# A hybrid decoder layer: fewer expert tiles ahead, and the router's queries in two passes

## The chip, the cores and the metric

The kernel runs on one core of a Trainium2 chip. It holds one layer of a decoder trunk for 512 tokens of width 2048 in float32. The metric is the device time of one execution in microseconds. The kernel before takes 3278.4 us (median of three runs, 3274.56 to 3291.7).

## What is computed

The layer adds two things to its input `h`: attention, and a layer of very small experts (PEER). A final norm follows. The change touches the second part alone. Per token it is:

```python
q = (xt @ w_query).reshape(T, 8, 2, 128)               # 8 heads, two halves
scores = jnp.einsum('thpc,hpnc->thpn', q, sub_keys)    # 128 keys for each half
vals, idx = lax.top_k(scores, 16)                      # of each half
cand = (vals[..., 0, :, None] + vals[..., 1, None, :]).reshape(T, 8, 256)
top_vals, top_c = lax.top_k(cand, 16)                  # 16 experts a head, 128 a token
experts = i1 * 128 + i2                                # of 16384
gates = softmax(top_vals)
hdn = gelu(einsum('ted,td->te', expert_down[experts], x))
y = einsum('ted,te->td', expert_up[experts], gates * hdn)
```

## The kernel before, in words

**Two ways to the experts.** Tokens come in four blocks of 128. The first 320 tokens go through *all* 16384 experts on TensorE, and a table `g_d` of gates, zero nearly everywhere, picks what counts. The last 192 tokens (64 of block 2, part "e", and all of block 3, part "g") are *gathered*: an indirect DMA on Pool (L511) brings one expert row for each of 128 partitions, 1 MB, and DVE multiplies and sums it (L517 for the down table, L525 for the up table). There are 384 such steps (`steps`, 64 down and 64 up for "e", 128 and 128 for "g"); four row buffers (`NROW`) hold what is under way.

**Weights in two halves.** Each float32 weight tile (128x1024, 512 KB) is rounded on ACT to a high part (L93) and the rest is a low part (L94, by DVE or Pool as `lo_on` says); `mm3` makes three matmuls of it (L99 to L101). A *down tile* is 128 experts: two pieces, 48 matmuls of 320 columns (`dn`), then Gelu into `hold`. An *up* step is 24 matmuls (`up`), 16 steps for a group of eight experts' tiles.

**Stages.** Behind attention, h is normed and transposed (`ht`). *Routing*: `queries(hp)` makes one half of one head's queries for all 512 tokens (48 matmuls of 512 columns, `pq`), the part for blocks 0 and 1 is set aside in `kept`; `choose(hh, b0, ...)` then searches two blocks on DVE (L541 to L545 top 16, L578 to L580 the one-hot lookup of the index). Calls for blocks 2 and 3 alternate with calls for blocks 0 and 1 one head behind. *One-hot stage*: for 40 groups of eight tokens, DVE makes two one-hot tiles (L673, L674), ACT scales one, PE multiplies them (`gm`, L680), ACT copies to `stg`, and SP writes `g_d`; one gather step goes with each group. Since PE has room there, `SPILL` = 28 down tiles (experts 100 to 127) are computed ahead and parked in DRAM (`hid_d`), and then ten more into the ten `hold` buffers. *Loop*: up steps for group g, one down tile every two steps, and gather steps by a rate (`due`, 1.6 a step while there are down tiles and 0.8 later, when `hold` is reloaded from `hid_d`). The last group of eight brings in the final norm.

**What sets the order.** The code is written in program order, and a scheduler places instructions on each engine by its own estimate, within what buffers and dependences allow. Every engine then works strictly in that order, and so does the queue of SP, which issues the loads: an instruction that waits holds all behind it.

Of the kernel before, what the change touches and what calls it, by code (L numbers as in the profile page):

```python
# [18 lines left out]
P = 128  # L19
# [10 lines left out]
PH = 8  # L30
# [14 lines left out]
ER = P // NE  # L45
EH = 128 // ER
HOLD = 10
SPILL = 28
NG = 8

PACE = mybir.DependencyInfo(mybir.DependencyClass.NoSync, mybir.DependencyReason.SCHED_ONLY)
# [8 lines left out]
def peer_block(ctx, tc, x, x_t, w_qk, w_v, w_fg, w_o, w_pq, sub_keys, down_t, down, up_t, up,  # L60
# [17 lines left out]
    ahead = []  # L78

    def fetch(src, pool):  # L80
        raw = pool.tile([P, 1024], F32, tag="raw", name="raw", bufs=3)
        DMA.dma_start(raw, src)
        return raw

    def load_split(src, lo_on=None, pool=None, bufs=2):

        pool = pool or wts
        raw = ahead.pop(0) if ahead else fetch(src, pool)
        if isinstance(raw, tuple):
            return raw  # L90
        hi = pool.tile([P, 1024], F32R, tag="hi", name="hi", bufs=bufs)
        lo = pool.tile([P, 1024], F32R, tag="lo", name="lo", bufs=bufs)
        A.activation(hi, raw, AF.Copy)  # L93
        (lo_on or V).tensor_tensor(lo, raw, hi.bitcast(F32), ALU.subtract)  # L94
        return hi, lo
# [343 lines left out]
    def aux(name):  # L439
        return psum.tile([P, S], F32, tag="aux", name=name, bufs=4)  # L440
# [91 lines left out]
    with tc.tile_pool(name="route", bufs=1, side="right") as rp:  # L532
# [57 lines left out]
                V.reciprocal(den, den)  # L590
                V.tensor_tensor(t, t, den.unsqueeze(2).broadcast_to([P, RB * PH, TK]), ALU.mult)

        kept = rp.tile([P, 2 * PH, RB * P], F32, name="kept")

        def queries(hp):
            ps = aux(f"pq{hp}")
            for piece in range(2):
                hi, lo = load_split(w_pq[hp, :, piece * 1024:(piece + 1) * 1024], G if hp else V)
                for kk in range(8):
                    k = piece * 8 + kk  # L600
                    sl = slice(kk * P, (kk + 1) * P)
                    mm3(ps, (hi[:, sl], lo[:, sl]), (hn[0][:, :, k], hn[1][:, :, k]), k == 0, k == NK - 1)
            qt = rp.tile([P, RB * P], F32, name="qt", bufs=2)
            A.copy(qt, ps[:, RB * P:])
            A.copy(kept[:, hp], ps[:, :RB * P])
            return qt


        for hh in range(PH):
            choose(hh, NB - RB, queries)  # L610
            if hh == PH - 1:
                for dst, src in ((gidx_e, ex), (gate_e, top)):
                    for r in range(ER):
                        V.tensor_copy(dst[r * NE:(r + 1) * NE], src[E0:, EB].rearrange("p h k -> p (h k)")[:, r * EH:(r + 1) * EH])
                V.tensor_copy(gidx, ex[:, GB])
                V.tensor_copy(gate_g, top[:, GB].rearrange("p h k -> p (h k)"))
            if hh:
                choose(hh - 1, 0, lambda hp: kept[:, hp])
        choose(PH - 1, 0, lambda hp: kept[:, hp])
    if "ex" in dbg:  # L620
        DMA.dma_start(dbg["ex"], ex)
        DMA.dma_start(dbg["gate"], top)
# [69 lines left out]
    with tc.tile_pool(name="exp", bufs=1, side="right") as xp:  # L692
# [110 lines left out]
        for g in range(NE1 // NG):  # L803
            pp = []
            for j in range(NG):
                e = g * NG + j
                ph, pl = (z[:, NGC:].rearrange("p c k t -> p (c k t)")[:, pslot * ND:(pslot + 1) * ND] for z in hn)
                pslot = (pslot + 1) % npslot
                A.activation(ph, hold[e], AF.Copy)
                V.tensor_tensor(pl, hold[e], ph.bitcast(F32), ALU.subtract)  # L810
                pp.append((ph, pl))
            for c in range(NK):
                uh, ul, _ = ups.pop(0)
                ps = aux("up")
                for j in range(NG):
                    mm = mm3(ps[:, :ND], (uh[:, j], ul[:, j]), pp[j], j == 0, j == NG - 1)
                up_split(g * NK + c + 1)
                if g == 0:
                    add = V.tensor_copy(yacc[:, c], ps[:, :ND])
                else:  # L820
                    add = V.tensor_tensor(yacc[:, c], yacc[:, c], ps[:, :ND], ALU.add)
                behind = ups[0][2] if ups else None
                if ups:
                    tc.add_manual_dep(add.ins, behind, PACE, reason="pace")
                e = HOLD + g * NG + c // 2
                if c % 2 and e < NE1:
                    if e < NE1 - SPILL:
                        down_tile(e, (V, V))
                    else:
                        hold[e] = hold_p.tile([P, ND], F32, tag="hold", name=f"hold{e}")  # L830
                        DMA.dma_start(hold[e], hid_d[e - (NE1 - SPILL)])
                if c % 2 and (g + 1) * NG + c // 2 < NE1:
                    gate_tile((g + 1) * NG + c // 2)
                due += 1.6 if e < NE1 - SPILL else 0.8
                while due >= 1:
                    gather_step(mm, behind)
                    due -= 1
                if g == NE1 // NG - 1 and c == NK - 1:
                    assert gstep[0] >= len(steps)
                if g == NE1 // NG - 2 and c == 4:  # L840
                    fin_load()
                if g == NE1 // NG - 1 and c % 4 == 3:
                    fin_quarter(c // 4)
# [74 lines left out]
```

## Time and profile before

| | |
|---|---|
| median of three runs | 3278.4 us |
| the profiled execution | 3290.1 us, its span 3288.3 us |
| mean granted TensorE clock | 0.976 |
| PE, DVE, ACT, POOL busy | 94%, 75%, 37%, 30% of the span |
| moved by DMA | 846 MB, 402.7 MB of it by the gathers |
| routing, one-hot stage | 966 to 1232 us, 1242 to 1478 us |
| loop from the first up step to the last down tile | 1642 to 2936 us |
| up steps alone, last group and norm | 2936 to 3288 us |

The table gives the stages by the times at which their first and last instructions stand. A busy share over the whole span hides that the bound changes from stage to stage; it is read stage by stage.

### The profile page before, as it was taken

What the parts mean: (1) busy time and instruction counts of PE and PEld (TensorE: products, weight loads), DVE (VectorE), ACT (ScalarE), POOL (GpSimd) and SP (SyncE); (2) the same over time, 40 slices, a digit from 0 to 9 for tenths busy, and PEclk for the clock granted to TensorE, in tenths of its full rate; (3) what the DMA queues carried; (4) which work ended last, traced back from release to release, by engine and by line L of the source; (5) the groups of instructions that cost most, each with busy time, mean ns of one, the idle gap of its engine ahead of it and who ended that gap; (6) DMA issues with size and microseconds to landing.
All of it is one profiled execution on the core that took longest, in us unless ns stands there. A gap on an engine that the chain in (4) does not pass through costs nothing.

```text
span 3288.3 us, 46948 instructions
## 1 busy us (share of the span) xinstructions
PE 3099.4 (94%) x18265; PEld 2830.5 (86%) x18265; DVE 2472.8 (75%) x3518; ACT 1211.2 (37%) x1849; POOL 971.8 (30%) x515
## 2 busy tenths in 40 slices
PE   6999999999999968889999998999999999998897
PEld 4887778878877767789999998999999999988887
DVE  5226665444348999980799998999999999988895
ACT  4224444343231127883333333333333333322233
POOL 2000000000013346775434433334434333432210
PEclk9999999999999998989999999999999999999998
DMA  4322222224442237986799999999999999999883
GB/s 179 101 93 75 69 69 73 66 66 129 134 135 71 77 122 256 339 325 235 279 387 392 395 404 333 405 406 379 386 402 404 404 395 406 383 380 361 326 328 123
DMA packets 215791, 846.49 MB, mean 257 GB/s; under 512 B 20944, under 2 KB 69456, under 8 KB 163216
## 3 DMA queue, kind: packets, MB, share of 16 engines
q1 hardware_dynamic: 159424, 439.37, 37.2%
q0 software_dynamic: 55296, 402.68, 30.8%
q8 instruction: 143, 2.34, 0.3%
q10 hardware_dynamic: 848, 1.44, 0.2%
q14 instruction: 80, 0.66, 0.1%
HBM read 806.31 MB, written 35.91 MB: 256 GB/s over the span
## 4 chain that ended last, share of the span: by engine, by line
PE 75%; DVE 12%; DMA 4%; POOL 4%; issue 4%; ACT 1%; ACTq 0%; SPq 0%; POOLq 0%; DVEq 0%
PE dn L99 8%; PE up L99 8%; PE dn L100 8%; PE up L100 7%; PE up L101 7%; PE dn L101 7%; PE mm L101 4%; PE mm L100 4%; PE mm L99 4%; POOL lo L94 2%; PE po L100 2%; PE po L99 2%; PE po L101 2%; PE gm L680 2%; PE pv L101 2%
## 5 line engine op out<-in xcount | busy, mean ns | idle before, releaser
L93 ACT ACTIVATE hi<-raw 128x1024 fp32r<-128x1024 f32 x416 | 440.4, 1059 | 750.7 <-PE dn L101 206.0
L99 PE MATMUL dn<-hn,lo 128*128 128x320 f32 x2048 | 653.6, 319 | 62.5 <-POOL lo L94 62.0
L99 PE MATMUL up<-hn,ulo 128*128 128x320 f32 x2048 | 645.6, 315 | 43.6 <-DVE ulo L797 43.4
L94 DVE TENSOR_TENSOR lo<-raw,hi 128x1024 fp32r<-128x1024 f32 x320 | 389.6, 1224 | 375.6 <-ACT hi L93 375.0
L100 PE MATMUL dn<-hn,hi 128*128 128x320 f32 x2048 | 647.7, 316 | 0.0
L100 PE MATMUL up<-hn,uhi 128*128 128x320 f32 x2048 | 640.3, 313 | 6.3 <-DVE hn L810 6.3
L101 PE MATMUL dn<-hn,hi 128*128 128x320 f32 x2048 | 645.6, 315 | 0.0
L101 PE MATMUL up<-hn,uhi 128*128 128x320 f32 x2048 | 639.1, 312 | 0.0
L796 ACT ACTIVATE uhi<-uraw 128x1024 fp32r<-128x1024 f32 x256 | 271.5, 1061 | 638.2 <-PE up L101 482.8
L99 PEld LDWEIGHTS dn<-hn,lo 128*128 128x128 f32 x2048 | 389.7, 190 | 74.0 <-POOL lo L94 72.4
L99 PEld LDWEIGHTS up<-hn,ulo 128*128 128x128 f32 x2048 | 390.4, 191 | 57.4 <-DVE ulo L797 52.9
L100 PEld LDWEIGHTS up<-hn,uhi 128*128 128x128 f32 x2048 | 390.8, 191 | 7.9 <-DVE hn L810 7.9
L101 PEld LDWEIGHTS up<-hn,uhi 128*128 128x128 f32 x2048 | 390.4, 191 | 0.0
L100 PEld LDWEIGHTS dn<-hn,hi 128*128 128x128 f32 x2048 | 390.1, 190 | 0.0
L101 PEld LDWEIGHTS dn<-hn,hi 128*128 128x128 f32 x2048 | 389.1, 190 | 0.0
L94 POOL TENSOR_TENSOR lo<-raw,hi 128x1024 fp32r<-128x1024 f32 x96 | 274.4, 2865 | 293.5 <-ACT hi L93 293.5
L797 DVE TENSOR_TENSOR ulo<-uraw,uhi 128x1024 fp32r<-128x1024 f32 x256 | 313.5, 1225 | 57.7 <-ACT uhi L796 57.5
L511 POOL DMA_INDIRECT rows<-in_up,gidx x128 | 214.5, 1676 | 408.4 <-DVE yg_g L525 392.4
L511 POOL DMA_INDIRECT rows<-in_down,gidx x128 | 227.2, 1775 | 357.7 <-DVE rows L517 324.7
L517 DVE SCALAR_TENSOR_TENSOR rows<-rows,hng_g 128x2048 f32<-128x2048 f32 x128 | 290.4, 2283 | 9.9 <-DMA rows<-in_down,gidx 5.9
L525 DVE SCALAR_TENSOR_TENSOR yg_g<-rows,coef_g,yg_g 128x2048 f32<-128x2048 f32 x127 | 297.7, 2344 | 0.0
L108 POOL TENSOR_TENSOR rstd_g<-ms_g,mhalf 128x4 f32<-128x4 f32 x2 | 2.0, 1016 | 685.5 <-DVE ms_g L106 685.5
(257 smaller groups left out, 5132.3 us busy)
## 6 DMA issues: line engine op xcount, KB each, us to landing
raw<-in_down_t SPq DMA_DIRECT2D x256, 512.0 KB
uraw<-in_up_t SPq DMA_DIRECT2D x256, 512.0 KB
raw<-in_w_qk SPq DMA_DIRECT2D x64, 512.0 KB
g_d<-stg SPq DMA_DIRECT2D x10, 2048.0 KB
gt<-g_d SPq DMA_DIRECT2D x32, 640.0 KB
raw<-in_w_v SPq DMA_DIRECT2D x32, 512.0 KB
raw<-in_w_o SPq DMA_DIRECT2D x32, 512.0 KB
raw<-in_w_pq SPq DMA_DIRECT2D x32, 512.0 KB
```

The source lines that it names most:

```text
L93: A.activation(hi, raw, AF.Copy)
L94: (lo_on or V).tensor_tensor(lo, raw, hi.bitcast(F32), ALU.subtract)
L99: PE.matmul(ps, a[1], b[0], start=first, stop=False)
L100: PE.matmul(ps, a[0], b[1], start=False, stop=False)
L101: return PE.matmul(ps, a[0], b[0], start=False, stop=last)
L108: G.tensor_tensor(r[:, :width], m[:, :width], mhalf[:, :width], ALU.pow)
L511: ld = G.indirect_dma_start(out=rows, out_offset=None, in_=table, in_offset=bass.IndirectOffsetOnAxis(ap=ix[:, j:j + 1], axis=0))
L517: use = V.scalar_tensor_tensor(rows, rows, 1.0, hng[part], ALU.mult, ALU.mult, accum_out=dots[part][:, j:j + 1])
L525: use = V.scalar_tensor_tensor(yg[part], rows, coef[part][:, j:j + 1], yg[part], ALU.mult, ALU.add)
L680: gm = PE.matmul(ps[:, t * P:(t + 1) * P], o2[:, qq * 4 + t], o1[:, qq * 4 + t], start=True, stop=True)
L796: A.activation(uh, raw, AF.Copy)
L797: sub = V.tensor_tensor(ul, raw, uh.bitcast(F32), ALU.subtract)
```

## The change

`SPILL` goes from 28 to 8: experts 120 to 127 are computed ahead, and the loop has down tiles up to 119. Queries are made twice: once for blocks 2 and 3, all heads, and then for blocks 0 and 1, so that `kept` is not needed, each matmul has 256 columns, and the query weights are loaded, rounded and subtracted in both passes. They have buffers of their own in the pool of routing (`rp`), two raw ones. In the first pass DVE makes the low part of each first piece and Pool of each second (both on DVE for the very first half); in the second Pool makes all but the first half's. The index lists of the gathered tokens are complete behind the first pass, and two gather steps follow each call of the second. The rate in the loop goes to 1.38 and 0.65 a step.

```diff
-SPILL = 28
+SPILL = 8
...
-        raw = pool.tile([P, 1024], F32, tag="raw", name="raw", bufs=3)
+        raw = pool.tile([P, 1024], F32, tag="raw", name="raw", bufs=3 if pool is wts else 2)
...
-        kept = rp.tile([P, 2 * PH, RB * P], F32, name="kept")
-
-        def queries(hp):
-            ps = aux(f"pq{hp}")
...
+        def queries(b0):
+
+            def of(hp):
+                ps = aux(f"pq{hp}{b0}")[:, :RB * P]
+                cg = slice(b0 * P // GC, (b0 + RB) * P // GC)
+                for piece in range(2):
+                    hi, lo = load_split(w_pq[hp, :, piece * 1024:(piece + 1) * 1024], G if hp and (piece or b0 == 0) else V, rp)
+                    for kk in range(8):
+                        k = piece * 8 + kk
+                        sl = slice(kk * P, (kk + 1) * P)
+                        mm = mm3(ps, (hi[:, sl], lo[:, sl]), (hn[0][:, cg, k], hn[1][:, cg, k]), k == 0, k == NK - 1)
+                qt = rp.tile([P, RB * P], F32, name="qt", bufs=2)
+                A.copy(qt, ps)
+                last[0] = mm
+                return qt
+            return of
...
         for hh in range(PH):
-            choose(hh, NB - RB, queries)
...
-            if hh:
-                choose(hh - 1, 0, lambda hp: kept[:, hp])
-        choose(PH - 1, 0, lambda hp: kept[:, hp])
+            choose(hh, NB - RB, queries(NB - RB))
...
+        for hh in range(PH):
+            choose(hh, 0, queries(0))
+            for _ in range(2):
+                gather_step(last[0])
...
-                due += 1.6 if e < NE1 - SPILL else 0.8
+                due += 1.38 if e < NE1 - SPILL else 0.65
```

What the scheduler makes of it, at three places. On PE, at the end of the one-hot stage, before (`gm` are the one-hot products, `dn` down tiles):

```order
L680 MATMUL gm<-o_10120,o_10119 128x128
L101 MATMUL dn_11185<-hn_6788,hi 128x320
L99 MATMUL dn_11185<-hn_6788,lo 128x320
L100 MATMUL dn_11185<-hn_6789,hi 128x320
L101 MATMUL dn_11185<-hn_6788,hi 128x320
```

And at the same place now:

```order
L683 MATMUL gm<-o_11105,o_11104 128x128 x8
L683 MATMUL gm<-o_11132,o_11131 128x128 x8
L683 MATMUL gm<-o_11159,o_11158 128x128 x8
L99 MATMUL up<-hn_6788,ulo 128x320
L100 MATMUL up<-hn_6789,uhi 128x320
```

Counted in that order, 809 matmuls of down tiles stood ahead of the last one-hot product, and 1015 more between it and the first up step. Now 138 stand ahead of the first query, 289 among the queries, 629 from there to the last one-hot product, and none between it and the first up step.

On DVE, just ahead of the low part of the first up weights, now (`rows` gather products, `hold` gate products, `ulo` the low part); before, the low part stood there without any gate product ahead of it:

```order
L517 SCALAR_TENSOR_TENSOR rows_12039,dots_e<-rows_12039,hng_e 128x2048
L785 TENSOR_TENSOR hold_11773<-hold_11773,gt_12375 128x320
L785 TENSOR_TENSOR hold_11839<-hold_11839,gt_12375 128x320
L785 TENSOR_TENSOR hold_11905<-hold_11905,gt_12375 128x320
L517 SCALAR_TENSOR_TENSOR rows_12105,dots_e<-rows_12105,hng_e 128x2048
L785 TENSOR_TENSOR hold_11971<-hold_11971,gt_12375 128x320
L785 TENSOR_TENSOR hold_12037<-hold_12037,gt_12377 128x320
L517 SCALAR_TENSOR_TENSOR rows_12171,dots_e<-rows_12171,hng_e 128x2048
L785 TENSOR_TENSOR hold_12103<-hold_12103,gt_12377 128x320
L785 TENSOR_TENSOR hold_12169<-hold_12169,gt_12377 128x320
L785 TENSOR_TENSOR hold_12235<-hold_12235,gt_12377 128x320
L517 SCALAR_TENSOR_TENSOR rows_12237,dots_e<-rows_12237,hng_e 128x2048
```

All eight gate products and the last gather products of part "e" for the down table now precede it.

On Pool, around the first gather steps, before:

```order
L94 TENSOR_TENSOR lo<-raw,hi 128x1024 x33
L511 DMA rows_9072<-in_down,gidx_e 128x2048
L511 DMA rows_9099<-in_down,gidx_e 128x2048
L511 DMA rows_9126<-in_down,gidx_e 128x2048
L511 DMA rows_9153<-in_down,gidx_e 128x2048
```

and now:

```order
L94 TENSOR_TENSOR lo<-raw,hi 128x1024 x29
L511 DMA rows_8690<-in_down,gidx_e 128x2048
L511 DMA rows_8693<-in_down,gidx_e 128x2048
L94 TENSOR_TENSOR lo<-raw,hi 128x1024 x2
L511 DMA rows_8883<-in_down,gidx_e 128x2048
L511 DMA rows_8886<-in_down,gidx_e 128x2048
L94 TENSOR_TENSOR lo<-raw,hi 128x1024 x2
L511 DMA rows_9076<-in_down,gidx_e 128x2048
```

The gather steps stand among the subtractions of the second pass; before they came behind all of the queries'.

## Rows read from the trace of the kernel before

**Rows 1.** The chain that ended last, by engine (the page's part 4).
```profile
PE 75%; DVE 12%; DMA 4%; POOL 4%; issue 4%; ACT 1%; ACTq 0%; SPq 0%; POOLq 0%; DVEq 0%
```
**Rows 2.** Busy time by stage: stretch, its length, engines, clock, DMA, GB/s.
```profile
core 0: us, PE busy (x) PEld busy (x) DVE busy (x) ACT busy (x) POOL busy (x), PEclk, DMA share, GB/s
966.00:1232.00 266.00, 225.76 (x1011) 180.81 (x1010) 243.31 (x956) 52.91 (x75) 105.33 (x40) 0.94 0.26 91
...
1242.00:1478.00 236.00, 196.41 (x1264) 186.58 (x1264) 216.53 (x157) 196.44 (x431) 171.87 (x65) 0.91 0.85 313
1478.00:1642.00 164.00, 158.45 (x1015) 152.03 (x1014) 61.27 (x50) 57.27 (x76) 84.59 (x41) 0.99 0.74 257
1642.00:2936.00 1294.00, 1282.49 (x8648) 1277.46 (x8647) 1208.68 (x1161) 446.08 (x548) 516.45 (x289) 1.00 1.00 393
2936.00:3203.00 267.00, 232.17 (x1443) 221.17 (x1441) 225.49 (x226) 76.51 (x99) 59.34 (x44) 0.94 0.92 340
3203.00:3272.00 69.00, 65.18 (x424) 63.16 (x425) 41.26 (x62) 23.27 (x36) 0.75 (x1) 0.95 0.36 115
```
**Rows 3.** Groups of instructions in routing, 966 to 1232 us: busy, mean ns.
```profile
L579 DVE TENSOR_TENSOR oh<-oh,cd 128x1728 f32<-128x1728 f32 x16 | 50.5, 3153 | 0.1
...
L541 DVE MAX8 vf<-sc 128x8 f32<-128x128 f32 x63 | 17.6, 282 | 21.8 <-PE sc L556 21.8
L561 DVE TENSOR_SCALAR vf<-ii 128x32 f32<-128x32 uint32 x32 | 17.3, 540 | 0.1
...
L94 POOL TENSOR_TENSOR lo<-raw,hi 128x1024 fp32r<-128x1024 f32 x36 | 101.5, 2823 | 159.6 <-ACT hi L93 159.6
```
**Rows 4.** Single instructions in routing: start us, us, engine and line.
```profile
1038.69 0.17 DVE L561 TENSOR_SCALAR vf<-ii 128x32 f32<-128x32 uint32 x1
...
1041.93 1.94 DVE L578 TENSOR_TENSOR oh<-iota_c,posf 128x1728 f32<-128x1728 f32 x1
...
1044.06 3.87 DVE L579 TENSOR_TENSOR oh<-oh,cd 128x1728 f32<-128x1728 f32 x1
...
1041.96 4.16 POOL L94 TENSOR_TENSOR lo<-raw,hi 128x1024 fp32r<-128x1024 f32 x1 [5.86 <-ACT hi L93]
1048.13 2.35 POOL L94 TENSOR_TENSOR lo<-raw,hi 128x1024 fp32r<-128x1024 f32 x1 [2.02 <-ACT hi L93]
...
1092.45 1.94 DVE L579 TENSOR_TENSOR oh<-oh,cd 128x1728 f32<-128x1728 f32 x1
```
**Rows 5.** Groups of instructions in the one-hot stage, 1242 to 1478 us.
```profile
L517 DVE SCALAR_TENSOR_TENSOR rows<-rows,hng_e 128x2048 f32<-128x2048 f32 x40 | 121.3, 3035 | 0.0
L674 DVE TENSOR_TENSOR o<-iota_e,i1t 128x1024 f32<-128x1024 f32 x39 | 54.0, 1384 | 0.0
...
L94 POOL TENSOR_TENSOR lo<-raw,hi 128x1024 fp32r<-128x1024 f32 x26 | 91.9, 3554 | 36.3 <-ACT hi L93 36.3
```
**Rows 6.** Groups of instructions on DVE in the loop, 1642 to 2936 us.
```profile
L517 DVE SCALAR_TENSOR_TENSOR rows<-rows,hng_g 128x2048 f32<-128x2048 f32 x128 | 290.4, 2283 | 9.9 <-DMA rows<-in_down,gidx 5.9 <-DMA hng_g<-hn_d 3.9
...
L94 DVE TENSOR_TENSOR lo<-raw,hi 128x1024 fp32r<-128x1024 f32 x179 | 216.2, 1219 | 41.7 <-ACT hi L93 41.4
```
**Rows 7.** Start of routing: a load in the chain, and SP's issues behind it.
```profile
959.36 4.83 DMA sk<-in_sub_keys
...
959.75 5.96 SPq L82 DMA_DIRECT2D raw<-in_w_pq  x2
```
**Rows 8.** End of the one-hot stage: issues on SP, then the first on DVE.
```profile
1478.78 0.33 SPq L685 DMA_DIRECT2D g_d<-stg  x1
...
1490.92 0.38 SPq L780 DMA_DIRECT2D gt<-g_d  x1
...
1507.39 2.57 DVE L797 TENSOR_TENSOR ulo<-uraw,uhi 128x1024 fp32r<-128x1024 f32 x1 [31.98 <-ACT uhi L796]
```
**Rows 9.** Stretches of the loop, columns as in rows 2.
```profile
1680.00:1980.00 300.00, 300.00 (x2036) 300.00 (x2035) 282.79 (x241) 105.90 (x131) 117.53 (x66) 1.00 1.00 398
1980.00:2040.00 60.00, 49.94 (x302) 46.42 (x301) 46.20 (x53) 17.27 (x24) 22.26 (x12) 0.91 0.92 329
```
**Rows 10.** A wait in the tail, 2936 to 3203 us: in total, times, longest.
```profile
DVE hold L782 <- DMA hold<-hid_d: 10.9, 1, 10.9
```
**Rows 11.** The rounding of a weight piece on ACT (the page's part 5).
```profile
L93 ACT ACTIVATE hi<-raw 128x1024 fp32r<-128x1024 f32 x416 | 440.4, 1059 | 750.7 <-PE dn L101 206.0
```

More of the change, by code (lines that the diff above doesn't have):

```diff
@@ L591, in choose @@
                 V.tensor_tensor(t, t, den.unsqueeze(2).broadcast_to([P, RB * PH, TK]), ALU.mult)
-        kept = rp.tile([P, 2 * PH, RB * P], F32, name="kept")
-        def queries(hp):
-            ps = aux(f"pq{hp}")
[L597 to L606, printed above, removed]
@@ L609, in peer_block @@
-        for hh in range(PH):
-            choose(hh, NB - RB, queries)
[L611 to L616, printed above, removed]
-            if hh:
-                choose(hh - 1, 0, lambda hp: kept[:, hp])
@@ new lines, in peer_block @@
+        last = [None]
+        for hh in range(PH):
+            choose(hh, NB - RB, queries(NB - RB))
+        for dst, src in ((gidx_e, ex), (gate_e, top)):
+            for r in range(ER):
+                V.tensor_copy(dst[r * NE:(r + 1) * NE], src[E0:, EB].rearrange("p h k -> p (h k)")[:, r * EH:(r + 1) * EH])
+        V.tensor_copy(gidx, ex[:, GB])
+        V.tensor_copy(gate_g, top[:, GB].rearrange("p h k -> p (h k)"))
+        for hh in range(PH):
+            choose(hh, 0, queries(0))
+            for _ in range(2):
+                gather_step(last[0])
```

## The prediction

> **What bounds the kernel now.** I read the chain that ended last first: three quarters of it is PE and an eighth DVE [rows 1]. A share over the span says little here, because the layer has stages with different limits, so I then cut the span into stages and read every engine's busy time, the granted clock and the DMA share in each [rows 2]. What the reader is to see there:
>
> From 966 to 1232 us (routing) DVE works 243 of 266 us: the top-16 searches set the pace. PE is busy beside it with the queries, Pool is at 105 us, the DMA engines at 0.26. From 1242 to 1478 (the one-hot stage that writes g_d) DVE works 217 of 236 us. From 1478 to 1642 only PE is full: it works off down tiles, 1015 matmuls. From 1642 to 2936 PE, DVE (1209 of 1294) and the DMA engines (1.00) are all full at once. From 2936 to 3203, when down tiles are used up, PE falls to 232 of 267. So before 1478 a microsecond is DVE's, after it PE's. From 3203 to 3272 is the last group of eight; 16 us of final norm end the span at 3288.3.
>
> A second thing is in the rows: DVE and Pool slow each other. The same product of two tiles takes 1.94 us at 1092 and 3.87 us at 1044, where a Pool subtraction overlaps it and itself takes 4.16 us [rows 4]. Over routing this makes L579 3.15 us instead of 1.94 (16 times, 19 us) and L561 0.54 instead of 0.17 [rows 4] (32 times, 12 us): 31 us for 36 Pool subtractions, 0.87 us each [rows 3]. In the one-hot stage it makes the gather's product 3.04 us where 2.28 is its time in the loop, and L674 1.38 where I take 1.22, the mean of DVE's own subtraction of that size [rows 5, 6]: 30 + 6 us for 26, 1.4 us each.
>
> **The change part by part.**
>
> *The start.* Query weights had been loaded during the output projection, in the buffers shared by all weights. Now they have two buffers of their own, in memory that becomes free late, and stand on SP behind the sub-keys, which are issued at 959.4 and need 4.8 us; before, the two weight loads behind them held SP for 6.0 us [rows 7]. Landed at about 967, rounded and subtracted by 970, 48 matmuls, copy and scores: the first search starts at about 978, not 966. **+12**. PE fills the wait with 138 matmuls of spilled tiles.
>
> *Routing.* Queries are as much PE work as before: 768 matmuls of 512 columns become 1536 of 256. The nearest row, 320 columns, gives 300 us / 2036 = 0.147 us [rows 9]; 256 columns cost between four fifths of that and all of it, 181 to 226 us. With 289 matmuls of down tiles (42 us) and the scores PE has at most 285 us of work, under DVE's. The 16 MB more of weights fall where the DMA engines are at 0.26: nothing, while that cover lasts. DVE is the bound and gets 18 more subtractions at 1.22 us (22 us) and 16 gather products at 2.28 and an accumulator read (38 us) [rows 6]. Pool's subtractions in this stretch go from 36 to 57 (45 for queries, 12 for down tiles); at 0.87 to 1.4 us of DVE each that is 50 to 81 us instead of 31. I take 1.0, near the lower end, since half of them stand in the first pass, which has no gather products: +26 (19 to 50). Of the 23 us in which DVE stood still, 21.8 were waits for scores [rows 3], in the first calls, at 512 columns; the pass at 256 columns hands over the first scores in half the time: 10 us stay. 978 + 243 + 22 + 38 + 26 + 10 = **1317** for the end of routing (1232 before).
>
> Beside a Pool subtraction L579 took about the sum of both, while L578, of two inputs too and beside the same one from 1041.96, stayed at 1.94 us [rows 4]. The Trainium skill, GPSIMD Engine Reference, section 8 (Key points), says that Pool shares its memory interfaces with VectorE and contends with every DVE instruction that has two SBUF inputs; the trace agrees for L579 and not for L578. What it would make of the time stands among the rivals.
>
> *What else moves, at nothing.* ACT rounds 32 pieces more, 34 us at 1.06 [rows 11], and is at 53 of 266 us there. Twenty tiles fewer go out to DRAM and back, 160 KB each. On SP each write of a spilled tile waits for its Gelu, with query loads queued behind: hidden while DVE has most of a call (about 15 us of work) ahead, and part of the rival of the two buffers if not.
>
> *One-hot stage.* 10 us of transition stay (1232 to 1242), and one subtraction, 1328. The stage holds 236 us with 26 Pool subtractions; now the order has 8, which returns 18 x 1.4 = 26 us, and 16 on DVE, which cost 20: 230 us. The 40 gather products are unchanged. It ends at **1558** (1478 before).
>
> *The edge behind it.* Before, 1015 matmuls of down tiles stood between the last one-hot product and the first up matmul, so that PE never saw what follows: the last g_d write is issued at 1478.8, the first table load behind it at 1490.9, and the low part of the first up weights, loaded behind that, starts on DVE at 1507.4 [rows 8]. Now nothing stands there (piece of the PE order above): PE waits for write, table, weights, then for DVE, which has eight gate products and three gather products ahead of the low part. Between 20 us (no gathers in the way, SP less crowded) and 45; I take 34, just over the 29 of the rows. First up matmul at **1592** (1642 before).
>
> *The loop.* 16 tiles more are left for it: 10368 matmuls up to the last down tile, 8640 before. At 0.147 us [rows 9] 1527 us, and the change from the first gathered block to the second, which costs 105 missing matmuls, 16 us, between 1980 and 2040: 1543, to 3135. Lower gather rate (1.38 for 1.6) relieves DVE and DMA, but PE was already full there; I take nothing for it.
>
> *The tail.* Up-only steps fall from 76 to 36. Before the last 16 of them, 60 took 267 us, 4.45 each for 24 matmuls of 0.147 = 3.5. Now 20: at 4.45 us 89, and the 10.9 us for the first reloaded tile [rows 10] is paid once whatever their number, as is the end of the gathered block, so 104. Last group and final norm stay, 85 us. 3135 + 104 + 85 = **3324**.
>
> Against the span of 3288.3 (executed 3290.1) this is +36: the loop starts 50 us earlier and the tail is 163 us shorter, but 1728 matmuls more make the loop 249 us longer. The median before, 3278.4, is 12 us under the profiled execution; I add the difference to it: **3314 us**.
>
> **The rivals.**
> *The port costs less, faster.* Pool's subtractions could fall beside MAX8 and index searches, whose rows show no loss. All 57 and 8 at nothing: routing ends 57 us earlier, the one-hot stage 11: 3314 - 68 = 3246. It passes to faster once 65 Pool subtractions cost DVE under 0.3 us each. For it: L578's 1.94. Against: L579's mean of 3.15, and more exposed products come in.
> *The port takes all, slower still.* Every Pool subtraction of routing meets a DVE product: 57 x 2.35 [rows 4] = 134 us, 77 over what I take: 3391. Of the two forms in [rows 4] one bears it out. This is what the page named above would give.
> *The losses are paid back, no change.* Port at 0.87 (-7), edge at 20 (-14), tail at 3.8 us a step (-13): 3280.
> *Two buffers are too few, slower still.* In the second pass a piece needs its load (at most the sub-keys' 4.8 us), rounding 1.06 [rows 11] and Pool 2.4 to 4.2: up to 10.1 us, with two buffers 20 us for four pieces, against DVE's 21 for a call. A gather issue or a down tile's subtraction ahead on Pool adds 2.8: 26 us a call, eight calls, +40: 3354. It decides where DVE waits for scores in the second pass.
> *The change doesn't do what it says:* if the gathers issued in the second pass arrived too late, DVE would stand before them, in order, with the searches behind; that is the row above at another queue, and priced with it.
>
> **How the numbers follow.** Forecast 0.42, two buffers 0.14, port takes all 0.05 (all three slower), no change 0.22, faster 0.17. A measurement of this kernel tells 0.5%, 16 us, from no change: faster 0.17, same 0.22, slower 0.61. The range takes the no-change case and the bounds of the port and the edge, 3256 to 3350.
>
> **What would show it.** Right: DVE over 95% busy from 980 to about 1315; first one-hot product near 1328 and last near 1558; a gap of about 34 us on PE behind it; first up matmul near 1592; the last down tile near 3135. L579 above 3 us in both passes. Wrong if routing ends before 1270, if up matmuls follow the last one-hot product within 15 us, or if the loop takes over 0.150 us a matmul.

## The result, and the profile after

The changed kernel takes 3339.2 us (median of four runs, 3336.7 to 3341.6). Beside it on the same chip the kernel before takes 3276.6 us. The ratio is 1.0156, with a 95% interval of 1.0127 to 1.0185: 1.6% slower. The forecast was 3314 us, in a range of 3256 to 3350. The profiled execution took 3336.7 us, its span is 3334.9 us, its mean granted clock 0.973.

The same cut into stages as in [rows 2], for the kernel after (stretch, its length, then the busy time and instructions of PE, PE's weight loads, DVE, ACT and POOL, the granted clock, the DMA share, GB/s):

```profile
985.00:1342.00 357.00, 279.71 (x1973) 267.81 (x1971) 342.51 (x1009) 100.79 (x123) 187.79 (x77) 0.90 0.52 174
1352.00:1566.00 214.00, 174.44 (x1166) 163.60 (x1164) 205.01 (x171) 189.65 (x426) 74.03 (x44) 0.97 0.88 329
1566.00:1607.00 41.00, 0.56 (x4) 0.36 (x3) 26.41 (x30) 7.50 (x14) 12.75 (x10) 0.53 0.95 362
1607.00:3165.00 1558.00, 1542.87 (x10376) 1537.75 (x10377) 1377.64 (x1322) 533.57 (x654) 489.54 (x307) 0.99 0.97 365
3165.00:3250.00 85.00, 74.88 (x484) 73.05 (x483) 66.60 (x72) 26.51 (x36) 13.26 (x11) 0.96 0.87 308
3250.00:3318.00 68.00, 61.92 (x419) 59.82 (x418) 49.08 (x66) 25.52 (x43) 1.48 (x1) 1.00 0.46 157
```

The stages stand in the same order: routing (DVE busy 342.5 of 357), the one-hot stage (205 of 214), a gap in which PE does nothing, the loop (PE 1543 of 1558), the up-only steps, the last group. Against the forecast, each at the time at which it was due:

| | before | forecast | after | forecast missed by, in this step alone |
|---|---|---|---|---|
| first search | 966 | 978 | 984.8 | +7 |
| end of routing | 1232 | 1317 | 1342.2 | +18 |
| last one-hot product | 1477.5 | 1558 | 1566.6 | -17 |
| first up matmul | 1641.7 | 1592 | 1607.4 | +7 |
| last down tile | 2936.3 | 3135 | 3165.2 | +15 |
| start of the last group | 3203.5 | 3239 | 3249.8 | -19 |
| end | 3288.3 | 3324 | 3334.9 | 0 |

Routing ended 110 us later than before, 19 of them from its later start. Of these, 21 came back in the one-hot stage and 123 in the work that used to stand behind it. Then the loop was 263 us longer and what follows it 182 us shorter. What follows asks which half of the change cost this, and whether the mechanisms named were the true ones.

**Routing, closer.** Groups of instructions in the routing stage after, 984 to 1342 us (busy us, mean ns | waited before, and for what); [rows 3] are those of before:

```profile
L94 POOL TENSOR_TENSOR lo<-raw,hi 128x1024 fp32r<-128x1024 f32 x58 | 155.3, 2689 | 128.0 <-ACT hi L93 127.7
L579 DVE TENSOR_TENSOR oh<-oh,cd 128x1728 f32<-128x1728 f32 x16 | 43.7, 2730 | 0.1
L517 DVE SCALAR_TENSOR_TENSOR rows<-rows,hng_e 128x2048 f32<-128x2048 f32 x16 | 41.4, 2590 | 0.0
L561 DVE TENSOR_SCALAR vf<-ii 128x32 f32<-128x32 uint32 x32 | 23.7, 741 | 0.4
L541 DVE MAX8 vf<-sc 128x8 f32<-128x128 f32 x64 | 17.7, 281 | 6.3 <-PE sc L556 6.1
L575 DVE CAST posf<-pos 128x32 f32<-128x32 uint32 x16 | 14.8, 924 | 0.1
L568 DVE TENSOR_TENSOR cd<-vf 128x64 f32<-128x64 f32 x16 | 11.3, 703 | 0.3
```

L579 is at 2.73 us, not at the 3.15 of before; what grew is small instructions. Taking each line's time alone from its shorter instances (for example L561 0.17 us, L575 0.18, L568 0.18, L579 1.94, L517 2.28), what the instructions that overlap work on Pool took beyond it (where that is over 0.3 us) sums to 28 us in the first pass and 44 in the second, 72.5 in all, against 34 before. For 58 Pool subtractions, 26 and 32 in the two passes, that is 1.25 us each. (The expectations below say 62 and 1.17: subtractions at the borders of stretches had been counted twice.) How that looks in the timeline (start, us):

```profile
1156.64 4.74 POOL L94 TENSOR_TENSOR lo<-raw,hi 128x1024 fp32r<-128x1024 f32 x2
...
1158.00 3.43 DVE L561 TENSOR_SCALAR vf<-ii 128x32 f32<-128x32 uint32 x1
...
1189.74 0.95 POOL L511 DMA_INDIRECT rows<-in_down,gidx_e  x1
1189.98 5.81 DVE L568 TENSOR_TENSOR cd<-vf 128x64 f32<-128x64 f32 x5
1190.70 4.70 POOL L94 TENSOR_TENSOR lo<-raw,hi 128x1024 fp32r<-128x1024 f32 x2
```

An instruction of 0.17 us stands from 1158.00 until 1161.43, and the second of the two subtractions ends at 1161.38. Five additions, some 1 us of work, take from 1189.98 to 1195.79. Taken singly, the second of them, 0.18 us alone, stood 5.34 us, from 1190.13 to 1195.47; the others kept their 0.2 us. It began while a gather's issue was at work, and two subtractions followed that one at once, the second of which ends at 1195.40. So DVE does not run slower beside Pool; it stands until Pool's instruction, or a run of them, is over. That also reads [rows 4] better than the prediction did: at 1041.93 L578 began 0.03 us ahead of Pool and kept its 1.94 us, while Pool's subtraction took 4.16, about 1.94 and 2.35; L579, which came behind Pool, stood until it ended and ran then. For these instructions who starts first decides, but not every kind is held. In the routing of both traces L579 was held in all 17 cases in which it began inside a Pool subtraction, the cast L575 in 10 of 11 and L561 in 20 of 24 (the five others began in its last 0.3 us). The reduction L580 (1.9 us) began so 10 times and the searches with MAX8 108 times, and none was held; MAX8 is at 0.281 us, as in [rows 3] (0.282).

The Trainium skill, SBUF — State Buffer, section "Who interferes with whom", says this: whoever issues first gets the shared pair of ports for the whole instruction, the other blocks, and scalar products and casts can be among those that ask for it. The trace agrees, with the 3.43 us of a 0.17 us instruction beside it. That one instruction stands through two subtractions, as the addition does that had begun 0.58 us ahead of the first of them, is beyond that sentence, and what lets it happen is not shown here.

**The gap, closer.** On SP, DVE and PE, 1567 to 1608 us (us of the step, its wait in brackets); [rows 8] is the same place before:

```profile
1567.88 0.33 SPq L688 DMA_DIRECT2D g_d<-stg  x1
...
1575.37 1.12 SPq L783 DMA_DIRECT2D gt<-g_d  x2
1576.53 19.23 SPq L796 DMA_DIRECT2D uraw<-in_up_t  x3
...
1596.23 1.29 DVE L785 TENSOR_TENSOR hold<-hold,gt 128x320 f32<-128x320 f32 x3 [9.67 <-DMA gt<-g_d]
...
1607.41 0.60 PE L99 MATMUL up<-hn,ulo 128*128 128x320 f32 x1 [40.86 <-DVE ulo L800]
```

The gate table is asked for at 1575.4 and is there at 1596.2. From there DVE has eight gate products and three gather products ahead of the low part, as foretold: 11 us. From the issue of the last write of the table (1567.9) to the first gate product it is 28 us. Of the 14.8 MB moved in these 41 us, 8.7 MB were gathers.

### The profile page after: what moved, and what is told of

Its sections match the earlier page's. It is cut to its first block, busy times and chain, and to the rows that moved or that the text cites. A ratio compares the mean times of both kernels' runs of the same rounds, so it can differ in the third digit from the quotient of the medians.

```text
span 3334.9 us, 48525 instructions
## 1 busy us (share of the span) xinstructions
PE 3090.7 (93%) x19033; PEld 2870.8 (86%) x19033; DVE 2546.8 (76%) x3575; ACT 1248.4 (37%) x1883; POOL 822.0 (25%) x490
## 4 chain that ended last, share of the span: by engine, by line
PE 50%; DVE 3%; ACT 2%; DMA 2%; issue 2%; POOL 0%; SPq 0%; ACTq 0%; DVEq 0%; POOLq 0%
PE up L99 8%; PE up L100 8%; PE up L101 8%; PE dn L100 8%; PE dn L99 8%; PE dn L101 8%; DMA uraw<-in_up_t 1%; ACT o L679 1%; PE gm L683 1%; ACT stg L686 1%; DVE ulo L800 0%; DMA rows<-in_down,gidx 0%; DVE o L677 0%; DVE yg_g L525 0%; DVE o L676 0%
## 5 line engine op out<-in xcount | busy, mean ns | idle before, releaser
L93 ACT ACTIVATE hi<-raw 128x1024 fp32r<-128x1024 f32 x448 | 473.1, 1058 | 777.6 <-PE dn L101 267.0
L94 DVE TENSOR_TENSOR lo<-raw,hi 128x1024 fp32r<-128x1024 f32 x377 | 467.6, 1243 | 355.9 <-ACT hi L93 355.5
L99 PE MATMUL dn<-hn,lo 128*128 128x320 f32 x2048 | 645.6, 315 | 33.5 <-DVE lo L94 25.7
L511 POOL DMA_INDIRECT rows<-in_down,gidx x128 | 207.4, 1620 | 459.8 <-DVE rows L517 426.6
L511 POOL DMA_INDIRECT rows<-in_up,gidx x128 | 194.2, 1517 | 486.9 <-DVE yg_g L525 466.3
L517 DVE SCALAR_TENSOR_TENSOR rows<-rows,hng_g 128x2048 f32<-128x2048 f32 x128 | 291.1, 2284 | 8.1 <-DMA rows<-in_down,gidx 5.9
L94 POOL TENSOR_TENSOR lo<-raw,hi 128x1024 fp32r<-128x1024 f32 x71 | 189.0, 2672 | 325.8 <-ACT hi L93 325.5
L99 PE MATMUL mm<-xn,lo 128*128 128x512 f32 x512 | 204.3, 399 | 0.0
```

The costliest lines, as they stand in the source:

```text
L99: PE.matmul(ps, a[1], b[0], start=first, stop=False)
L511: ld = G.indirect_dma_start(out=rows, out_offset=None, in_=table, in_offset=bass.IndirectOffsetOnAxis(ap=ix[:, j:j + 1], axis=0))
L517: use = V.scalar_tensor_tensor(rows, rows, 1.0, hng[part], ALU.mult, ALU.mult, accum_out=dots[part][:, j:j + 1])
```

## The experiments

Spans and moments are from each run's profiled execution; ratios are against the kernel before, run beside it. "Left" counts the matmuls of down and up from the first up matmul on. At 0.1473 us each [rows 9] they give a time; the rest of the span is what the tail and the loop's stalls add.

| run | ratio (95%) | end of routing | first up | left | their time | rest | span |
|---|---|---|---|---|---|---|---|
| before | 1 | 1232 | 1642 | 10464 | 1541 | 105 | 3288.3 |
| after | 1.0156 (1.0127 to 1.0185) | 1342 | 1607 | 11232 | 1654 | 73 | 3334.9 |
| lo_act | 1.0012 (0.9993 to 1.0031) | 1293 | 1564 | 11232 | 1654 | 77 | 3295.8 |
| no_early_gathers | 1.0029 (1.0012 to 1.0047) | 1297 | 1562 | 11232 | 1654 | 82 | 3298.1 |
| lo_dve | 1.0136 (1.0099 to 1.0173) | 1377 | 1600 | 11232 | 1654 | 78 | 3333.2 |
| spill8_alone | 0.9915 (0.9890 to 0.9939) | 1235 | 1515 | 11400 | 1679 | 67 | 3260.5 |
| passes_alone | 1.0147 (1.0102 to 1.0192) | 1362 | 1652 | 10728 | 1580 | 103 | 3335.2 |
| twice15 | 1.0154 (1.0116 to 1.0192) | 1361 | 1636 | 10920 | 1609 | 97 | 3341.1 |
| single17 | 0.9924 (0.9900 to 0.9948) | 1238 | 1520 | 11256 | 1658 | 83 | 3260.5 |
| twice_quiet | 1.0123 (1.0087 to 1.0160) | 1344 | 1597 | 11218 | 1652 | 74 | 3322.7 |
| quiet8 | 0.9839 (0.9813 to 0.9864) | 1234 | 1497 | 11304 | 1665 | 82 | 3243.1 |

### Pool's part in routing (lo_act)

In the changed kernel, the low parts that Pool made of query weights are copied by ACT:

```diff
-hi, lo = load_split(..., G if hp and (piece or b0 == 0) else V, rp)
+hi, lo = load_split(..., A if hp and (piece or b0 == 0) else V, rp)
...
+        if lo_on is A:
+            A.activation(lo, raw, AF.Copy)
```

> The changed kernel, but the 45 low parts of query weights that Pool made are a copy made by ACT, so that their subtraction is left out and scores come from wrong low parts; everything else is the same work. Theory A (Pool's subtractions stretch DVE's instructions, 1.17 us of DVE for each: 72.5 us of stretched instructions beside 62 subtractions in the routing stage of the changed kernel): about 17 Pool subtractions are left, so that DVE loses 20 us instead of 72; routing ends near 1290 instead of 1342, the first up matmul stands near 1555 instead of 1607, and the time is about 3290 (3280 to 3305). Theory B (the calls of the second pass take 26 us because their pieces come too late through two buffers, or because of the gathers): routing still ends between 1330 and 1345, calls of the second pass stay above 25 us, and the time is 3330 to 3340.

Routing of this run, and its groups (three lines further down in the code: L582 is L579, L564 is L561, L578 is L575, L571 is L568, L544 is L541):

```profile
985.00:1293.00 308.00, 260.98 (x1928) 253.67 (x1928) 281.68 (x1009) 137.40 (x165) 55.41 (x31) 0.92 0.58 198
```

```profile
L97 POOL TENSOR_TENSOR lo<-raw,hi 128x1024 fp32r<-128x1024 f32 x12 | 33.3, 2779 | 129.7 <-ACT hi L93 129.6
L582 DVE TENSOR_TENSOR oh<-oh,cd 128x1728 f32<-128x1728 f32 x16 | 33.0, 2065 | 0.0
L564 DVE TENSOR_SCALAR vf<-ii 128x32 f32<-128x32 uint32 x32 | 9.5, 297 | 0.3
L578 DVE CAST posf<-pos 128x32 f32<-128x32 uint32 x16 | 3.8, 236 | 0.0
L544 DVE MAX8 vf<-sc 128x8 f32<-128x128 f32 x64 | 18.2, 285 | 24.4 <-PE sc L559 24.4
```

Routing ended at 1293 (expected 1290), the time fell by 1.4%, to that of the kernel before. L579 is at 2.07 us in place of 2.73, L561 at 0.30 in place of 0.74, the cast at 0.24 in place of 0.92: DVE's busy time is 61 us less for 46 Pool subtractions less, 1.3 us each. Routing got only 49 us shorter, since there is a new wait: DVE stands 24.4 us for scores, 6.3 in the kernel after. Theory B falls as far as the buffers go: here seven of the eight calls of the second pass take 17 to 23 us, and the first 28. The trace of after had already spoken against it: in the whole second pass DVE waited 0.3 us for scores, while four of its eight calls took 26 to 27 us and the others 17 to 23. What the gathers do is asked next.

### The early gather steps (no_early_gathers)

```diff
         for hh in range(PH):
             choose(hh, 0, queries(0))
-            for _ in range(2):
-                gather_step(last[0])
...
-                due += 1.38 if e < NE1 - SPILL else 0.65
+                due += 1.46 if e < NE1 - SPILL else 0.65
```

> The changed kernel without the two gather steps behind each call of the second pass; they come later, at a rate of 1.46 a step in the loop. Theory A (each step's product and accumulator read lie on DVE, which bounds the routing stage, so they are on the path there, 16 x 2.36 = 38 us, and beside PE's bound later they are free; the stretch by Pool's subtractions stays at about 1.1 us each): routing ends near 1300 instead of 1342, calls of the second pass take about 20 to 22 us, the first up matmul stands near 1565, the time is about 40 us under the changed kernel, 3300. Theory B (calls of the second pass are long because their pieces come late through two buffers): they stay above 25 us and the time moves by less than 15 us. Theory C (the steps must be done somewhere, DVE is as full in the loop, so what routing gains the loop gives back): routing ends near 1300, but the loop from the first up matmul to the last down tile is 25 to 40 us longer than 1557, and the time is 3325 to 3340.

Routing ended at 1297, calls of the second pass took 17 to 22 us, the time was 1.3% less than the changed kernel's. The loop, with 16 more steps in it, took 1561.9 us where after has 1557.8: theory C falls, DVE had room for them there. Of the 45 us, 4 are the first pass's and 40 the second's. That pass lost the steps' own 38 us, and it stood less behind Pool, 31 us in place of 44 for the same 32 subtractions; the two together would be some 12 us more than it gained, which I cannot place. The longest stands, in after and in twice15, are all of one form: a DVE instruction begins while a gather's issue is at work, subtractions follow that issue without a break, and DVE stands through the whole run, 5.34 us at 1190.13 in after and 7.60 us for an addition behind three subtractions in twice15. Here 4 gather issues stand in the second pass, in after 19. That the issues alone lowered the 44 us to 31 is not shown, since the 16 products they feed are gone too, and these had stood as well. Each of lo_act and no_early_gathers brought the time back to that of the kernel before; both together were not run.

### Low parts on DVE instead of Pool (lo_dve)

```diff
-hi, lo = load_split(..., G if hp and (piece or b0 == 0) else V, rp)
+hi, lo = load_split(..., V, rp)
```

> The changed kernel with all low parts of the query weights made by DVE. The scheduler then lets Pool work for down tiles instead, so 28 to 31 Pool subtractions are left in the routing stage (62 before) and DVE has 78 subtractions there instead of 18. Theory A (a Pool subtraction costs DVE 1.17 us by stretching, one on DVE 1.22): 60 x 1.22 = 73 us more and some 33 x 1.17 = 39 us less, routing ends near 1376 instead of 1342; the one-hot stage has no Pool subtractions and few down tiles, about 205 us; first up matmul near 1630; the time is about 20 us over the changed kernel. Theory B (Pool's subtractions cost DVE nothing): routing ends near 1415 and the time is 60 us or more over the changed kernel.

Its routing and its one-hot stage, and the two groups of subtractions in routing:

```profile
984.00:1376.00 392.00, 347.85 (x2495) 336.84 (x2494) 367.33 (x1067) 124.52 (x151) 80.27 (x39) 0.96 0.55 187
1384.00:1564.00 180.00, 124.23 (x640) 116.11 (x640) 179.16 (x161) 165.14 (x398) 91.03 (x40) 0.76 0.89 338
```

```profile
L94 DVE TENSOR_TENSOR lo<-raw,hi 128x1024 fp32r<-128x1024 f32 x78 | 110.4, 1415 | 14.3 <-ACT hi L93 14.3
L94 POOL TENSOR_TENSOR lo<-raw,hi 128x1024 fp32r<-128x1024 f32 x20 | 55.6, 2785 | 192.9 <-ACT hi L93 192.8
```

Routing ended at 1377 (expected 1376), with 60 subtractions more on DVE and some 38 fewer on Pool: DVE's busy time is 25 us more there. Sixty subtractions at 1.22 us are 73, so the 38 gave back some 48, about 1.3 us each: one on Pool costs DVE about what one on DVE does. But the time is the changed kernel's (1.0136 and 1.0156, intervals that overlap), not 20 us more: down tiles had moved into routing (the scheduler put 783 of their matmuls among the queries), the one-hot stage had neither them nor Pool's subtractions and took 180 us in place of 215. I had priced that stage at 205. So what DVE lost in routing here, 34 us, it was given back in the one-hot stage, 35.

### Fewer tiles alone (spill8_alone) and two passes alone (passes_alone)

The kernel before with 8 tiles, and the changed one with 28:

```diff
-SPILL = 28
+SPILL = 8
...
-                due += 1.6 if e < NE1 - SPILL else 0.8
+                due += 1.46 if e < NE1 - SPILL else 0.65
```

```diff
-SPILL = 8
+SPILL = 28
...
-                due += 1.38 if e < NE1 - SPILL else 0.65
+                due += 1.5 if e < NE1 - SPILL else 0.75
```

> The kernel before with 8 tiles ahead in DRAM in place of 28, its queries still in one pass (rate of gather steps 1.46 and 0.65, since none go early). Theory A (what counts is how many matmuls of down tiles lie beside DVE's stages, and how many are left behind them): routing ends at 1232 as before; 840 matmuls of down tiles stand up to the last one-hot product and only 48 behind it, so the gap of about 41 us behind that product shows, first up matmul near 1511; 11400 matmuls are left, 1679 us, and a tail with 20 up-only steps ahead of the last group instead of 60 saves some 37 us: 25 us faster than before, about 3252 (3240 to 3265). Theory B (fewer tiles ahead make the whole thing slower, whatever the queries do, because the loop gets 20 tiles longer): 3300 or more, near the changed kernel's 3339.

> The changed kernel with 28 tiles ahead again, queries in two passes (rate of gather steps 1.5 and 0.75). Theory A: routing ends near 1342 as in the changed kernel; 922 matmuls of down tiles then stand beside the one-hot stage, which PE bounds at about 230 us instead of 214, and 208 matmuls (31 us) behind it fill most of the gap; first up matmul near 1622; 10728 matmuls are left, 1580 us, and the long tail of 60 steps is back: about 25 us over the kernel before, 3302 (3295 to 3320). So each half of the change would be worth less than the whole costs, with opposite signs. Theory B (the two passes cost nothing, fewer tiles do): 3275 to 3285.

Routing, one-hot stage and gap; first the kernel before with 8 tiles, then two passes with 28:

```profile
969.00:1235.00 266.00, 225.80 (x1012) 180.84 (x1010) 243.44 (x958) 52.93 (x75) 105.29 (x40) 0.94 0.28 91
1244.00:1473.00 229.00, 195.50 (x1298) 184.94 (x1296) 218.49 (x168) 198.42 (x438) 125.09 (x56) 0.94 0.85 321
1473.00:1514.00 41.00, 9.14 (x48) 8.61 (x48) 23.82 (x27) 8.63 (x15) 12.15 (x10) 0.66 0.97 358
```

```profile
986.00:1361.00 375.00, 304.29 (x2121) 290.40 (x2120) 361.69 (x1007) 107.61 (x132) 211.47 (x85) 0.92 0.55 178
1371.00:1612.00 241.00, 200.26 (x1341) 187.65 (x1339) 239.55 (x159) 202.79 (x438) 154.06 (x68) 0.95 0.87 319
1612.00:1651.00 39.00, 33.58 (x207) 32.51 (x206) 19.57 (x18) 14.19 (x18) 14.17 (x8) 0.91 0.97 350
```

Fewer tiles alone make the kernel 0.85% faster, 28 us, as the ledger had it (25). Two passes alone cost 1.5%, 48 us, twice what I expected. So the two halves have opposite signs, and the whole slowdown is that of the passes. They do not add up either: -28 and +48 would be +20, measured is +51. With two passes, 8 tiles or 28 is the same time.

The table says why. In one pass, going from 28 to 8 brings the first up matmul forward by 127 us, leaves 936 matmuls more (138 us) and shortens the rest by 38. In two passes it comes forward by only 44, for 504 matmuls more (74 us) and 30 of rest. The stages of two passes are long enough to hide more down tiles: up to the last one-hot product the order of passes_alone has 1352 matmuls of them, that of after 1056, that of before 809. Taking tiles away there takes work out of time that is spent anyway.

### More tiles with two passes (twice15), more with one (single17)

```diff
-SPILL = 8
+SPILL = 15
```

```diff
-SPILL = 28
+SPILL = 17
```

with the rates at 1.42 and 0.68, and at 1.52 and 0.72.

> The changed kernel with 15 tiles ahead instead of 8 (rate of gather steps 1.42 and 0.68): 866 matmuls of down tiles beside the one-hot stage instead of 633 and 72 in the gap behind it. Theory A (at 8 tiles PE has nothing to do in 40 us behind the last one-hot product and stands for some 40 us beside that stage, so more tiles ahead are free there): 312 matmuls fewer are left for the time behind, 46 us; the tail has 14 steps more, 13 us: about 29 us under the changed kernel, 3310 (3300 to 3320). Theory B (the gap is the path of the gate table and the weights through DMA, and a PE with work in it only moves the same wait): no change, 3335 to 3343.

> The kernel before with 17 tiles ahead and queries in one pass (rate 1.52 and 0.72). The ledger says: first up matmul (1475 + the gap of 41, with 223 matmuls of down tiles, 33 us, inside it) near 1516; 11256 matmuls left at 0.1473 us, 1658 us; 67 us for the tail of 8 tiles and 1.8 us for each of nine more, 83: a span near 3257, that is 3 us under the run with 8 tiles ahead (3260.5), so no difference that can be told from it. A theory that the gap's idle time is lost work would give 25 to 30 us less, 3230 to 3235.

twice15 took the changed kernel's time, as theory B had it, but not for theory B's reason. The gap stayed at 41 us with 72 matmuls inside, and 312 fewer were left behind it. What ate the gain stands ahead of it: routing ended at 1361 in place of 1342, the one-hot stage took 225 us in place of 215, and the rest grew by 24 where I had 13. Groups of its routing, 984 to 1361 us:

```profile
L94 POOL TENSOR_TENSOR lo<-raw,hi 128x1024 fp32r<-128x1024 f32 x66 | 181.1, 2758 | 133.3 <-ACT hi L93 133.0
L517 DVE SCALAR_TENSOR_TENSOR rows<-rows,hng_e 128x2048 f32<-128x2048 f32 x16 | 53.5, 3346 | 0.0
L568 DVE TENSOR_TENSOR cd<-vf 128x64 f32<-128x64 f32 x16 | 15.9, 995 | 0.4
```

More tiles brought Pool more subtractions into the second pass (40 there, in place of 32), and the gather's product went from 2.59 to 3.35 us, the additions from 0.70 to 1.0: 68 us beyond the instructions' own times in that pass, 44 in the changed kernel's. My expectation, and that for passes_alone too, had left routing at 1342. That a tile put ahead costs DVE through Pool's port was a price I knew, and I did not charge it.

single17 came out at the time of 8 tiles in one pass (0.9924 and 0.9915, with the same span), as its ledger said: between 8 and 17 tiles what is hidden in the gap is lost again in the tail.

### What the gap is made of (quiet8, twice_quiet)

In the kernel before with 8 tiles, and in the changed one, the ten gather steps that go with the ten tiles for `hold` are left to the loop (rates 1.51 and 0.65, 1.43 and 0.65):

```diff
         for e in range(HOLD):
-            mm = down_tile(e, (G, V))
-            gather_step(mm)
+            down_tile(e, (G, V))
```

> The kernel before with 8 tiles ahead, queries in one pass, as in the run with 8 tiles alone, and without the ten gather steps of the ten tiles that go to the hold buffers: those ten stand later (rate 1.51 and 0.65). It asks what the gap of 41 us between the last one-hot product and the first up matmul is made of. Theory A (the gate table and the first up weights share the DMA engines with the gathers, which moved 10 of 17 MB there): the gap falls to 25 to 32 us, the first up matmul stands near 1502, and the time is 10 to 28 us under that run, about 3240. Theory B (the gap is the chain of write, read and load with its fixed times, whatever else moves): it stays at 38 to 42 us and the time within 8 us of that run's.

> The changed kernel without the ten gather steps of the ten tiles that go to the hold buffers (rate 1.43 and 0.65), the same edit as in the run that made the gap fall from 42 to 25 us with queries in one pass. Theory A (gathers take the DMA engines from the gate table and the first up weights): the gap behind the last one-hot product falls from 41 to 25 to 28 us, routing and the one-hot stage stay as they are, and the time is 14 to 18 us under the changed kernel. Theory B (in that run the gap was filled by 138 matmuls of down tiles, not shortened): here only 14 stand there, the gap stays near 40 us and the time does not move.

The gap of quiet8 in SP's issues and DVE's first gate product, then as a stretch; behind it the gap of twice_quiet:

```profile
1472.71 0.33 SPq L685 DMA_DIRECT2D g_d<-stg  x1
...
1484.26 1.10 SPq L779 DMA_DIRECT2D gt<-g_d  x2
...
1490.30 1.69 DVE L781 TENSOR_TENSOR hold<-hold,gt 128x320 f32<-128x320 f32 x4 [2.46 <-DMA gt<-g_d]
```

```profile
1471.00:1496.00 25.00, 20.90 (x142) 20.64 (x140) 10.60 (x17) 11.43 (x19) 0.30 (x1) 0.98 0.90 320
```

```profile
1571.00:1596.00 25.00, 3.34 (x12) 3.34 (x13) 5.96 (x13) 6.55 (x15) 1.71 (x2) 0.58 0.83 276
```

From issue to DVE the table took 6 us in quiet8, 21 in after, but in quiet8 it was issued later behind the last write (11.6 us, in after 7.5), so that the two are better compared from that write on: 17.6 us to the first gate product in quiet8 and 17.9 in twice_quiet, 28.4 in after. No gather product stands ahead of the first low part any more, and DVE's work there takes 6 us in place of 11. The gap fell from 41 to 25 us in both kernels, with 138 matmuls inside it and with 14. So it was the gathers, some 10 us on the way of the table and 5 us as products on DVE; the chain of write, read and load is the other 25 us. twice_quiet's span is 12 us under the changed kernel's (expected 14 to 18); the ratios, 1.0123 and 1.0156, have intervals that overlap, so that in two passes the gain is not clear of the noise. In one pass it is: quiet8 is 1.6% faster than the kernel before (0.9839, with 8 tiles alone 0.9915, and these intervals lie apart) and the fastest of all that ran. It is the kernel before with two small edits: 8 tiles ahead instead of 28, and ten gather steps moved out of the stretch in which the gate table is on its way, with the rate in the loop set to match.

## Why the prediction came out as it did

The sign, the bound of each stage and the chain of causes held; the number was 25 us low. Of these, 11 are in the sum (3324 for the span, 3334.9 measured), the net of terms that missed by up to 19 each. The other 14 are my last step: I took the profiled execution of before to be 12 us over its median and carried that over, but that of after was 2.5 us under its own. The runs of before in the later comparisons lie between 3277 and 3303 us, so that difference was the spread of single runs and belonged in the range, not in the sum.

*The start* (+12 forecast, +19 measured). The mechanism held: the first query waited for its weights behind the sub-keys. They were issued at 964.4, five microseconds later than before, which I had not read from the order.

*Routing* (1317, measured 1342). Three terms. The start, 7. The port: 57 subtractions at 1.0 us were 57 us; it was 58 and 72.5 us, 1.25 each: 15. And DVE's waits, 10 forecast, about 15. The 22 us of subtractions and 38 of gather products are near what they took in the trace: 18 subtractions 26.8 us, 5 of them standing behind Pool, and 16 products 41.4, again 5 of them standing. The cause I named was shown by lo_act. I had counted L578 of [rows 4] as a case against the port; the 4.16 us of the Pool subtraction beside it make it one for the port, with Pool as the side that waited. The rival in which Pool's subtractions are paid in full had 134 us there and is further off. I took the price near the lower end "since half of them stand in the first pass, which has no gather products"; the first pass lost 1.1 us for each, and the second 1.4. What stands there is not the products of 2 us alone but also scalar products, casts and additions of 0.2 us that come while Pool is at work, so that fewer products are no protection. That also undid one of my signs: L579 was to be above 3 us in both passes, and it was at 2.77 and 2.69, while the small instructions grew.

*Two buffers are too few.* Four calls of 26 to 27 us came, the number that rival had (the mean of the eight was 23.6), and its condition was not met: DVE waited 0.3 us for scores in the second pass. The same calls were DVE's own work and its standing behind Pool. By its price alone this rival would have been taken for right; the condition written beside it told.

*One-hot stage* (230, measured 215). The gather's products went back to 2.28 us each, all 30 us of their stretch, where I had 26 us for everything; and the stage had had 19 us of idle DVE time, of which 10 went too. The product in that stage, 1352 to 1566 us; [rows 5] has it before:

```profile
L517 DVE SCALAR_TENSOR_TENSOR rows<-rows,hng_e 128x2048 f32<-128x2048 f32 x39 | 89.0, 2281 | 3.3 <-DMA rows<-in_down,gidx_e 3.3
```

*The edge* (34, measured 41). The parts were right: table, weights, then eight gate and three gather products. Their lengths were taken from a place where the DMA engines had less to do: here ten gathers were issued in 41 us, and twice_quiet shows that the gathers made 15 us of it, 5 of these as products on DVE.

*The loop* (1543, measured 1558). The price of a matmul held: from 1680 to 1900 us 1494 matmuls took 220 us, 0.1473. Fifteen microseconds were lost in the first 73:

```profile
1607.00:1680.00 73.00, 64.68 (x390) 62.59 (x390) 68.81 (x63) 18.70 (x22) 26.13 (x19) 0.91 1.00 392
1680.00:1900.00 220.00, 220.00 (x1494) 220.00 (x1493) 196.64 (x170) 77.29 (x95) 74.47 (x43) 1.00 0.97 366
```

There PE stood 8 us, nearly all of it for low parts of up weights from DVE, which was busy 69 of 73 us, and its 390 matmuls were 7 us longer than at 0.1473, at a granted clock of 0.91. The gathers in the gap are a small part of this, since twice_quiet lost 11 us at the same place without them. Before, the down tiles behind the one-hot stage had covered that start; I named nothing for it. At 0.1502 us a matmul over all, the bound that I set for being wrong (0.150) was just passed, by this start and not by the rate.

*The tail* (104 for 20 steps, measured 85). A step took 4.2 us with its wait for the reloaded tile inside it (7.0 us, once), not 4.45 and 10.9 more. Both [rows 10] and the 4.45 came from the same stretch, and I counted that wait twice: with the 4 us for the end of the gathered block, which that stretch holds as well, 15 of the 19 us.

So the forecast was near because its misses offset each other: 25 us late at the end of routing, 17 back in the one-hot stage, 22 lost at the edge and in the start of the loop, 19 back in the tail.

## What to carry to other kernels

Where DVE sets the pace, an elementwise instruction given to Pool is not free: here it cost DVE 0.9 to 1.7 us for each 128 x 1024 subtraction, about as much as doing it there. So price the two engines as one. Where work is put ahead into stages with another bound, count what is hidden up to the last moment of that bound, and what is left behind it: first up matmul, matmuls left at their price, and a rest of 67 to 105 us for the tail and the stalls set every run here side by side, those that missed too. And take changes of two parts apart before judging either: here one half was a gain (0.85%), and with a smaller edit beside it the gain came to 1.6%.

## What the runs showed of the hardware that I had not expected

- A DVE instruction of 0.17 us stood 3.43 us, and one of 0.18 us stood 5.34 us, until the Pool instructions beside them had ended. An instruction of 0.2 us can lose as much as one of 2 us; MAX8 and the index searches, 0.28 us each, and the reduction L580, 1.9 us, are not held.
- A gather's issue on Pool goes with this: the 32 subtractions of the second pass cost DVE 44 us with 19 gather issues and their 16 products among them, and 31 us with 4 issues and no products. Which of the two it was is not shown.
- From the issue of the table's last write until DVE has what is read back takes 18 us with few gathers in flight and 28 beside ten of them, at 362 GB/s in the whole. On the queue of SP the loads behind it wait as well: three weight loads held SP for 19.2 us.
- In the 41 us in which PE has next to no work its granted clock is 0.53, about the lower of its two levels, 1.2 GHz; behind it the first matmuls of the loop start 0.27 us apart (1608.40, 1608.66, 1608.93) in place of 0.147.
